# Conditioning-matrix products in bursts of two slabs, with an eight-buffer raw ring, in a conditioned hybrid decoder step

## The chip, the core and the metric

One Trainium2 chip, one of its cores. The metric is the device time of one execution of the whole step in microseconds (us), as the median of several runs. An execution that the profiler recorded supplies the rows; its span is the time from its first to its last instruction.

## The reference, cut to what matters

One decoder layer and a final RMSNorm are applied to 256 prompt tokens and 8 single-token samples. The nine modulation vectors (`mod`) come from the conditioning vector `c` through one large matrix, `ada_w` (2048 x 18432), here called the conditioning matrix.

```python
mod = (jax.nn.silu(c) @ ada_w + ada_b).reshape(n, N_SUBLAYERS, N_MOD, 1, D_MODEL)
h = modulate(rmsnorm(x, ffn1_norm), mod[:, 0, 0], mod[:, 0, 1])
x = x + FFN_RES * mod[:, 0, 2] * swiglu(h, ffn1_w_gate, ffn1_w_up, ffn1_w_down)
h = modulate(rmsnorm(x, mix_norm), mod[:, 1, 0], mod[:, 1, 1])
proj = h @ w_in
...
mixed = jnp.concatenate([y_ssm.reshape(n, l, D_SSM), y_pool], axis=-1).astype(x.dtype)
x = x + mod[:, 1, 2] * (mixed @ w_out)
h = modulate(rmsnorm(x, ffn2_norm), mod[:, 2, 0], mod[:, 2, 1])
x = x + FFN_RES * mod[:, 2, 2] * swiglu(h, ffn2_w_gate, ffn2_w_up, ffn2_w_down)
```

All arithmetic is float32. Between `w_in` and `w_out` one half of the channels goes through a state-space mixer (called S5) and the other through a pooling mixer.

## The kernel before

**Tokens and weights.** The 256 prompt tokens and 8 samples stand together as 264 moving columns. The weights (gate, up and down of both feed-forward blocks, `w_in`, `w_out`) are streamed once from HBM in slabs of 128 x 1024 float32 (512 KB), each of which holds eight 128 x 128 weight tiles. To keep float32 accuracy a slab is split into a high and a low part (`Stream.split`, lines 186 to 196: ScalarE copies to `hi`, line 190; VectorE computes `lo` = raw - hi, line 192), and each tile is multiplied in three passes: hi by Xh, hi by Xl, lo by Xh (`mm3`, lines 404 to 406). A weight slab is thus 24 matmuls of 264 columns.

**The conditioning matrix.** Its slabs go through the same stream but are not split. `sc` holds silu(c) as a stationary operand of 32 columns, and the slab itself is the moving operand. Four matmuls, each to its own group of 32 array columns and 32 PSUM partitions, make one step. For modulations 2 to 8 (`ada_step`, line 304) a step takes one of the 16 slices of the contraction, 2048 columns wide, which arrive as two 512 KB slabs; so here one slab of the title is a pair of DMAs, 7 x 16 = 112 of them. For modulations 0 and 1 (`ada0_step`, line 317) the columns are cut into five stages (`STG`), so that the first feed-forward block can begin before the whole of them is there: 8, 8, 16, 16 and 16 slabs of 512 KB. After the last slice VectorE transposes the PSUM tile (line 314 or 333) and `ada_fin` adds the bias; there is one PSUM tile for this work (`psa`, bufs=1), so the next modulation waits for the transposition of the last.

**Order.** All slabs, weights ("w") and conditioning ("a", and "b" for the further DMAs of a step), stand in one list, `ent`, in the order in which they are used. `Stream` issues their DMAs on SyncE's queue (SP) into a ring of 5 raw buffers; entry i waits until entry i-5 was used. When the matmuls need a further weight slab, `prep` first carries out every "a" entry that stands before it:

```python
    def fill(self):
        while self.dma < len(self.entries) and (self.dma < self.rb or self.used[self.dma - self.rb]):
            ...
    def prep(self):
        while self.is_ada():
            self.ada()
```

Up to three split slabs are kept ready. `w_units` and the table `pos` spread the conditioning steps over the weight slabs: in the first feed-forward block one step to some three weight slabs (modulations 4, 3, 2, 5), in the mixer stage (`win`, `wout`) one to some 1.3 (modulations 7, 6), in the beginning of the second block one to some 2.3 (modulation 8). The framework that builds the program may reorder instructions on an engine by its own plan, except where `keep_in_program_order` or a manual schedule forbids it.

**The S5 part** (`s5_v`, `s5_e`, `s5_y`) runs inside the second half of `win`: VectorE and ScalarE copy `u` into `V` (line 982), TensorE makes `E` from it (line 998), VectorE scans.

Of the kernel before, what the change touches and what calls it, by code (L numbers as in the profile page):

```python
# [21 lines left out]
KT = D // P  # L22
# [22 lines left out]
FV = 10  # L45
FIN = ((0, 1), (1, 1), (2, 2), (10, 2), (4, 2), (6, 2), (12, 2), (8, 2), (14, 2))
SG = 4
N1 = 3
STG = ((0, 2), (2, 4), (4, 8), (8, 12), (12, 16))

# [33 lines left out]
def ada0_units(s):  # L84
    a, b = STG[s]
    n = b - a
    if n == 1:
        return [((kt, kt + 1, kt + 2, kt + 3), (0, 1)) for kt in range(0, KT, 4)]
    if n <= 2:
        return [((kt, kt + 1), (0, 1)) for kt in range(0, KT, 2)]  # L90
    if n <= 4:
        return [((kt,), (0, 1)) for kt in range(KT)]
    return [((kt,), (i,)) for i in range(2) for kt in range(KT)]
# [116 lines left out]
def build(nc, tc, I, O):  # L210
    ctx = ExitStack()
    V, A, T, GP = nc.vector, nc.scalar, nc.tensor, nc.gpsimd
# [22 lines left out]
    wp = ctx.enter_context(tc.tile_pool(name="wp", bufs=1))  # L235
# [5 lines left out]
    def pt(shape, name, dt=F32):  # L241
        return pers.tile(list(shape), dt, tag=name, name=name)
# [33 lines left out]
    sc = pt([P, KT, 32], "sc")  # L276
# [18 lines left out]
    def ada_fin(at, mi, k0, k1):  # L295
        m = mods[mi][:, k0:k1, :]
        nk = k1 - k0
        add(m, at.rearrange("p (k b) -> p k b", b=32)[:, :, 0:NM], ada_b[:, mi, k0:k1].unsqueeze(2).broadcast_to([P, nk, NM]))
        if mi % 3 == 1:
            stt(m, m, 1.0, norms[:, mi // 3, k0:k1].unsqueeze(2).broadcast_to([P, nk, NM]), ALU.add, ALU.mult)  # L300
        elif mi in (2, 8):
            ts(m, m, 0.25)

    def ada_step(raws, mi, kt, stage):
        key = (mi, stage)
        if kt == 0:
            ada_ps[key] = psa.tile([P, 512], F32, tag="ada", name=f"ada{mi}_{stage}")
        ps = ada_ps[key]
        for j in range(4):
            T.matmul(ps[32 * j:32 * j + 32, :], lhsT=sc[:, kt, :], rhs=raws[j // 2][:, (j % 2) * 512:(j % 2 + 1) * 512],  # L310
                     start=(kt == 0), stop=(kt == KT - 1))
        if kt == KT - 1:
            at = wp.tile([P, 512], F32, tag="adaT", name=f"adaT{mi}_{stage}", bufs=1)
            V.transpose(out=at, in_=ps)  # L314
            ada_fin(at, mi, 0, KT)

    def ada0_step(raws, s, kts, ms):
        a, b = STG[s]
        n = b - a
        w = 32 * n  # L320
        if kts[0] == 0 and ms[0] == 0:
            ada_ps[s] = psa.tile([P, 512], F32, tag="ada", name=f"ada0_{s}")
        ps = ada_ps[s]
        r = raws[0][:, 0:len(kts) * len(ms) * 4 * w].rearrange("p (t m j c) -> p t m j c", t=len(kts), m=len(ms), j=4)
        for t, kt in enumerate(kts):
            for j in range(4):
                o = ps[32 * j:32 * j + 32, ms[0] * w:(ms[-1] + 1) * w].rearrange("p (m c) -> p m c", c=w)
                mm = T.matmul(o, lhsT=sc[:, kt, :], rhs=r[:, t, :, j, :], start=(kt == 0), stop=(kt == KT - 1))  # L328
                if s == 0:
                    tc.keep_in_program_order(mm)  # L330
        if kts[-1] == KT - 1 and ms[-1] == 1:
            at = wp.tile([P, 512], F32, tag="adaT", name=f"adaT0_{s}", bufs=1)
            tr = V.transpose(out=at[:, 0:2 * w], in_=ps[:, 0:2 * w])
            if s == 0:
                tc.keep_in_program_order(tr)
            for i in range(2):
                ada_fin(at[:, w * i:w * i + w], i, a, b)
            hooks["stage"](s)

    hooks = {}  # L340
    ent = []

    def ada_units(mi, kt):
        ent.append(("a", I["ada"][mi - 2, kt, 0], 2, (ada_step, mi, kt, None)))
        ent.append(("b", I["ada"][mi - 2, kt, 1]))

    def ada0_unit(s, i):
        ent.append(("a", I[f"ada0_{s}"][i], 1, (ada0_step, s) + ada0_units(s)[i]))

    def w_units(names, steps, first, last):  # L350
        us = [I[name][u] for name in names for u in range(I[name].shape[0])]
        pos = [first + (last - first) * i / max(1, len(steps)) for i in range(len(steps))]
        si = 0
        for u, ap in enumerate(us):
            while si < len(steps) and pos[si] <= u:
                ada_units(*steps[si])
                si += 1
            ent.append(("w", ap))
        while si < len(steps):
            ada_units(*steps[si])  # L360
            si += 1

    def steps(*ms):
        return [(mi, kt) for mi in ms for kt in range(KT)]

    for i in range(len(ada0_units(0))):
        ada0_unit(0, i)
# [3 lines left out]
    for s in range(len(STG) - 1):  # L371
        nu = SM * 2 * (STG[s][1] - STG[s][0]) // CH
        na = len(ada0_units(s + 1))
        k = 0
        for u in range(nu):
            if s == 0 and u == 0:
                ent.append(("w", I["w1"][u0 + u]))
            while k < na and k * (nu - 1) <= u * na:
                ada0_unit(s + 1, k)
                k += 1  # L380
            if s > 0 or u > 0:
                ent.append(("w", I["w1"][u0 + u]))
        while k < na:
            ada0_unit(s + 1, k)
            k += 1
        u0 += nu
    pos = {}
    s_a = steps(4, 3, 2, 5)
# [2 lines left out]
    for u in range(u0, n1):  # L391
        for s in pos.get(u, []):
            ada_units(*s)
        ent.append(("w", I["w1"][u]))
# [2 lines left out]

    for q in range(4):
        nc.sync.dma_start(out=x[:, 4 * q:4 * q + 4, :], in_=I["x"][:, 4 * q:4 * q + 4, :])
    st = Stream(nc, wp, ent, 5, 3)  # L400

    def mm3(ps, w, xh, xl, start, stop):
        hi, lo = w
# [266 lines left out]
    def first_block(pool, gh, gl, rb, n):  # L670
        pe2 = pse.tile([P, 2, 512], F32, tag="E", name=f"fe{cnt[0]}", bufs=1)
        pss = [bank() for _ in range(n - 2)] + [pe2[:, 0], pe2[:, 1]]
        for kt in range(KT):
            for ps in pss:
                mm3(ps[:, 0:NX], st.get(), gh[kt], gl[kt], kt == 0, kt == KT - 1)
            if kt == 2:
                rstd(rb)
        out = []
        for i, ps in enumerate(pss):
            g = pool.tile([P, N], F32, tag=f"fb{i}", name=f"fb{cnt[0]}_{i}", bufs=1)  # L680
            s8 = pool.tile([P, NM], F32, tag=f"fs{i}", name=f"fs{cnt[0]}_{i}", bufs=1)
            A.copy(out=s8, in_=ps[:, N:NX])
            mul(g, ps[:, 0:N], rb)
            A.activation(out=g[:, 0:SEQ], in_=g[:, 0:SEQ], func=AF.Identity, bias=s8[:, 0:1])
            add(g[:, SEQ:N], g[:, SEQ:N], s8[:, 1:9], GP)
            out.append(g)
        return out
# [57 lines left out]
    def ffn(shift, gs, gate, nm, first, gx, after):  # L745
        with ExitStack() as es:
# [5 lines left out]
            if first:  # L752
                def mid():
                    for _ in range(N1):
                        st.ada()
# [124 lines left out]
    with tc.tile_pool(name="mix", bufs=1) as mp:  # L880
        mixed = mp.tile([P, KT, N], F32, tag="mixed", name="mixed")
        with tc.tile_pool(name="poolp", bufs=1) as qp:
# [53 lines left out]
            pss = first_block(qp, X1[0], X1[1], rb, FBI)  # L936
            for a in range(0, KT, SG):
                for kt in range(a, a + SG):
                    one(kt)
                samples(a, a + SG)  # L940
            tc.keep_in_program_order(nc.sync.dma_start(out=pw, in_=I["poolw"]))

            def u_tile(hook=None):
                ps = bank()
                for kt in range(KT):
                    mm3(ps[:, 0:N], st.get(), Xh[:, kt, 0:N], Xl[:, kt, 0:N], kt == 0, kt == KT - 1)
                    if hook is not None:
                        hook(kt)
                return ps
# [6 lines left out]
            for mt in range(FBI, 8):  # L956
                ps = u_tile()
# [5 lines left out]
            ps = u_tile()  # L963
# [4 lines left out]
        with tc.tile_pool(name="s5p", bufs=1) as sp:  # L968
# [100 lines left out]
            for ft in range(1, NFT):  # L1069
# [5 lines left out]
                ps = u_tile(hook)  # L1075
# [30 lines left out]
            while plan:  # L1106
                a = plan.pop(0)
# [36 lines left out]
    with tc.tile_pool(name="fin", bufs=1) as fp:  # L1144
        rb = fp.tile([P, N], F32, tag="rb", name="rbf")
        rbp = rstd(rb)
        for a, n in FIN:
            o = fp.tile([P, 2, N], F32, tag="o", name=f"o{a}", bufs=len(FIN))
            for i in range(n):
                kt = a + i  # L1150
# [90 lines left out]


def program(L):
    nc = bacc.Bacc("TRN2", target_bir_lowering=False, num_devices=1)
    I = {k: nc.dram_tensor(k, a.shape, F32, kind="ExternalInput").ap() for k, a in L.items()}
    O = {k: nc.dram_tensor(k, s, F32, kind="ExternalOutput").ap() for k, s in OUTS.items()}
    with tile.TileContext(nc) as tc:
        build(nc, tc, I, O)
    nc.finalize()
    return nc  # L1250
# [21 lines left out]
```

## Time and profile before

| | |
|---|---|
| median of 3 runs | 2087.66 us (2086.51 to 2089.89) |
| span of the profiled execution | 2090.6 us, mean granted TensorE clock 0.986 of full |
| TensorE matmul (PE), busy | 2033.3 us, 97% of the span |
| VectorE (DVE), ScalarE (ACT), GpSimd (POOL) | 58%, 40%, 20% |
| DMA | 476 MB, 228 GB/s on average; queues q1 and q10 (hardware_dynamic, of SP and ScalarE), q8 and q14 (instruction) |

The profiled execution's own time is its span, 2090.6 us; the page shows nothing outside it, and it stands 2.9 us above the median of the runs. Busy shares of PE count a matmul until its modelled end, so that neighbours overlap; what a stream of matmuls costs is read from the distance of their starts. A matmul with float32 operands (the conditioning products) stands in the records twice, the three-pass ones once. A releaser behind an arrow (`<-`) is what ended the idle time before the row.

### The profile page before, as it was taken

The numbers are of one execution on the slowest core, as the hardware profiler recorded it, in microseconds if no ns is written. First come the engines' busy times: TensorE is split into PE (matmuls) and PEld (weight loads), VectorE is DVE, ScalarE is ACT, GpSimd is POOL, SyncE is SP. The second block draws the span as 40 slices with busy tenths as digits, with TensorE's granted clock in tenths as the row PEclk, the third lists the DMA queues.
The fourth block names the chain that finished last, engine by engine and source line by source line (L and its number), as shares of the span: only waits on it lengthen the run. The fifth ranks groups of instructions, "written<-read, shape, count | busy, mean of one in ns | idle before, by whom it ended". The sixth has DMA issues, their size and how long they took to land.

```text
span 2090.6 us, 41113 instructions
## 1 busy us (share of the span) xinstructions
PE 2033.3 (97%) x16856; PEld 1870.3 (89%) x16856; DVE 1212.7 (58%) x1978; ACT 842.3 (40%) x1258; POOL 410.6 (20%) x713
## 2 busy tenths in 40 slices
PE   6999999999999999999988899999999999999997
PEld 5788999899999989998766698899999999999997
DVE  4665855754444454467789776545555555554555
ACT  4332434433333333355445355433334333334343
POOL 0000100330764068043345332000000000000012
PEclk9999999999999999999989999999999999999998
DMA  8888777777676776777844656875555555555552
GB/s 321 314 296 286 246 261 252 286 267 250 229 247 231 258 252 234 267 261 251 314 151 178 219 205 219 283 273 182 180 175 180 182 187 175 182 182 175 179 181 103
DMA packets 135292, 476.43 MB, mean 228 GB/s; under 512 B 15160, under 2 KB 20152, under 8 KB 134840
## 3 DMA queue, kind: packets, MB, share of 16 engines
q1 hardware_dynamic: 134384, 473.07, 64.6%
q8 instruction: 132, 2.16, 0.4%
q10 hardware_dynamic: 720, 0.75, 0.1%
q14 instruction: 56, 0.46, 0.1%
HBM read 471.20 MB, written 3.01 MB: 227 GB/s over the span
## 4 chain that ended last, share of the span: by engine, by line
PE 71%; issue 11%; POOL 8%; DVE 7%; DMA 2%; ACT 1%; SPq 0%; POOLq 0%; ACTq 0%; DVEq 0%
PE mm L404 22%; PE mm L406 21%; PE mm L405 21%; PE ada_None L310 3%; POOL xu L215 2%; DVE lo L192 2%; PE ada L328 2%; POOL yt L215 1%; DVE V L982 1%; POOL X L215 1%; DMA raw<-ada 1%; POOL acc L215 1%; POOL h L215 1%; DVE S L215 1%; PE E L998 1%
## 5 line engine op out<-in xcount | busy, mean ns | idle before, releaser
L192 DVE TENSOR_TENSOR lo<-raw,hi 128x1024 fp32r<-128x1024 f32 x591 | 733.5, 1241 | 610.4 <-ACT hi L190 584.5
L190 ACT CAST hi<-raw 128x1024 fp32r<-128x1024 f32 x592 | 619.7, 1047 | 1000.6 <-PE mm L405 777.9
L404 PE MATMUL mm<-Xh,hi 128*128 128x264 f32 (+1 forms) x3168 | 922.8, 292 | 2.4 <-ACT Xh L735 1.7
L405 PE MATMUL mm<-Xl,hi 128*128 128x264 f32 (+1 forms) x3168 | 910.6, 288 | 0.0
L406 PE MATMUL mm<-Xh,lo 128*128 128x264 f32 (+1 forms) x3168 | 906.6, 287 | 1.7 <-DVE lo L192 1.5
L404 PEld LDWEIGHTS mm<-Xh,hi 128*128 128x128 f32 x3168 | 600.6, 190 | 77.3 <-issue 59.8
L406 PEld LDWEIGHTS mm<-Xh,lo 128*128 128x128 f32 x3168 | 602.8, 191 | 8.8 <-issue 5.6
L405 PEld LDWEIGHTS mm<-Xl,hi 128*128 128x128 f32 x3168 | 602.5, 190 | 7.9 <-issue 7.6
L404 PE MATMUL mm<-ah,hi 128*128 128x264 f32 x1408 | 404.3, 287 | 0.0
L406 PE MATMUL mm<-ah,lo 128*128 128x264 f32 x1408 | 400.7, 285 | 0.0
L405 PE MATMUL mm<-al,hi 128*128 128x264 f32 x1408 | 398.8, 283 | 0.0
L404 PEld LDWEIGHTS mm<-ah,hi 128*128 128x128 f32 x1408 | 264.9, 188 | 21.0 <-issue 15.9
L405 PEld LDWEIGHTS mm<-al,hi 128*128 128x128 f32 x1408 | 265.3, 188 | 0.0
L406 PEld LDWEIGHTS mm<-ah,lo 128*128 128x128 f32 x1408 | 264.7, 188 | 0.0
L215 POOL TENSOR_TENSOR acc<-acc,sq 128x264 f32<-128x264 f32 x42 | 45.8, 1089 | 748.5 <-ACT sq L655 748.5
L310 PE MATMUL ada_None<-raw,sc 128*32 128x512 f32 x896 | 129.0, 608 | 8.2 <-DVE adaT_None L314 5.0
L232 DVE SCALAR_TENSOR_TENSOR x<-mm,mod,x 128x256 f32<-128x256 f32 x78 | 37.6, 482 | 42.1 <-PE mm L406 42.1
L215 DVE TENSOR_TENSOR s<-s,mm 128x264 f32<-128x264 f32 x68 | 29.1, 428 | 55.7 <-PE mm L406 55.7
L328 PE MATMUL ada<-raw,sc 128*32 128x256 f32 (+1 forms) x640 | 43.8, 374 | 14.0 <-DMA raw<-ada 13.9
L215 POOL TENSOR_TENSOR xu<-X,apow 128x128 f32<-128x128 f32 x96 | 53.6, 579 | 3.8
L215 POOL TENSOR_TENSOR s<-s,partBuT 128x264 f32<-128x264 f32 x7 | 5.3, 755 | 219.4 <-DVE partBuT L215 203.0
L310 PEld LDWEIGHTS ada_None<-raw,sc 128*32 128x32 f32 x896 | 19.3, 108 | 29.8 <-DMA raw<-ada 9.3
(303 smaller groups left out, 1471.6 us busy)
## 6 DMA issues: line engine op xcount, KB each, us to landing
raw<-w SPq DMA_DIRECT2D x528, 512.0 KB, 3.8
raw<-ada SPq DMA_DIRECT2D x288, 512.0 KB, 5.2
raw<-win SPq DMA_DIRECT2D x32, 512.0 KB, 5.1
raw<-wout SPq DMA_DIRECT2D x32, 512.0 KB, 4.3
x<-x SPq DMA_DIRECT2D x4, 528.0 KB, 5.7
xin<-x SPq DMA_DIRECT2D x16, 132.0 KB, 3.7
y<-o SPq DMA_DIRECT2D x7, 264.0 KB, 2.7
Cm<-Cm SPq DMA_DIRECT2D x1, 1024.0 KB, 5.8
```

The costliest lines, as they stand in the source:

```text
L190: c = self.nc.scalar.copy(out=hi, in_=raw)
L192: e.tensor_tensor(out=lo, in0=raw, in1=hi.bitcast(F32), op=ALU.subtract)
L215: return e.tensor_tensor(out=out, in0=a, in1=b, op=op)
L232: return e.scalar_tensor_tensor(out=out, in0=a, scalar=s, in1=b, op0=op0, op1=op1)
L310: T.matmul(ps[32 * j:32 * j + 32, :], lhsT=sc[:, kt, :], rhs=raws[j // 2][:, (j % 2) * 512:(j % 2 + 1) * 512], start=(kt == 0), stop=(kt = ...
L328: mm = T.matmul(o, lhsT=sc[:, kt, :], rhs=r[:, t, :, j, :], start=(kt == 0), stop=(kt == KT - 1))
L404: T.matmul(ps, lhsT=hi, rhs=xh, start=start, stop=False)
L405: T.matmul(ps, lhsT=hi, rhs=xl, start=False, stop=False)
L406: T.matmul(ps, lhsT=lo, rhs=xh, start=False, stop=stop)
L982: e(out=v[32 * tau:32 * tau + 32, q, 64 * tau:64 * tau + n], in_=u[32 * q:32 * q + 32, 0:n])
L998: T.matmul(E[:, ri, q * 72:(q + 1) * 72], lhsT=bx[:, ri, q].rearrange("p a b -> p (a b)"), rhs=v[:, q, 192:N], start=True, stop=True)
```

## The change

`AB = 2` steps of the conditioning product now make one entry of the stream: `ada_step` takes four DMAs and does eight matmuls in a row, `ada0_steps` takes two slabs in a row (the first stage keeps single ones). The lists of steps are halved (`steps`), so that a burst comes after twice as many weight slabs. The ring of raw buffers grows from 5 to 8, which takes 12 KB more of each SBUF partition; for this the scratch for DMA descriptors is set to 1024 bytes.

```diff
+AB = 2
+RB = 8
...
-    def ada_step(raws, mi, kt, stage):
+    def ada_step(raws, mi, k0, stage):
...
-        for j in range(4):
-            T.matmul(ps[32 * j:32 * j + 32, :], lhsT=sc[:, kt, :], rhs=raws[j // 2][:, (j % 2) * 512:(j % 2 + 1) * 512],
-                     start=(kt == 0), stop=(kt == KT - 1))
-        if kt == KT - 1:
+        for kt in range(k0, k0 + AB):
+            for j in range(4):
+                T.matmul(ps[32 * j:32 * j + 32, :], lhsT=sc[:, kt, :],
+                         rhs=raws[2 * (kt - k0) + j // 2][:, (j % 2) * 512:(j % 2 + 1) * 512],
+                         start=(kt == 0), stop=(kt == KT - 1))
+        if k0 + AB == KT:
...
+    def ada0_steps(raws, s, i):
+        for r, u in zip(raws, ada0_units(s)[i:]):
+            ada0_step(r, s, *u)
...
     def ada_units(mi, kt):
-        ent.append(("a", I["ada"][mi - 2, kt, 0], 2, (ada_step, mi, kt, None)))
-        ent.append(("b", I["ada"][mi - 2, kt, 1]))
-
-    def ada0_unit(s, i):
-        ent.append(("a", I[f"ada0_{s}"][i], 1, (ada0_step, s) + ada0_units(s)[i]))
+        us = [I["ada"][mi - 2, k, h] for k in range(kt, kt + AB) for h in range(2)]
+        ent.append(("a", us[0], len(us), (ada_step, mi, kt, None)))
+        ent.extend(("b", u) for u in us[1:])
+
+    def ada0_unit(s, i, n=1):
+        ent.append(("a", I[f"ada0_{s}"][i], n, (ada0_steps, s, i)))
+        ent.extend(("b", I[f"ada0_{s}"][j]) for j in range(i + 1, i + n))
...
     def steps(*ms):
-        return [(mi, kt) for mi in ms for kt in range(KT)]
+        return [(mi, kt) for mi in ms for kt in range(0, KT, AB)]
...
             while k < na and k * (nu - 1) <= u * na:
-                ada0_unit(s + 1, k)
-                k += 1
+                ada0_unit(s + 1, k, AB)
+                k += AB
...
-    st = Stream(nc, wp, ent, 5, 3)
+    st = Stream(nc, wp, ent, RB, 3)
...
-    nc = bacc.Bacc("TRN2", target_bir_lowering=False, num_devices=1)
+    nc = bacc.Bacc("TRN2", target_bir_lowering=False, num_devices=1, dynamic_dma_scratch_size=1024)
```

The diff shifts the line numbers below it, by up to ten: lines 310, 314, 328, 404 and 982 of the kernel before are 313, 318, 336, 414 and 992 of the changed one. Three places show what the program makes of it.

TensorE, first feed-forward block, the first step of modulation 4 (`ada_None` is its PSUM tile, each row two matmuls; `mm` the accumulator of a weight product). Before:

```order
L405 MATMUL mm_2585<-Xl,hi_2498 128x264
L406 MATMUL mm_2585<-Xh,lo_2499 128x264
L310 MATMUL ada_None<-raw_2434,sc 32x512 x2
L310 MATMUL ada_None<-raw_2468,sc 32x512 x2
L404 MATMUL mm_2599<-Xh,hi_2532 128x264
L405 MATMUL mm_2599<-Xl,hi_2532 128x264
```

In the changed program:

```order
L415 MATMUL mm_2591<-Xl,hi_2504 128x264
L416 MATMUL mm_2591<-Xh,lo_2505 128x264
L313 MATMUL ada_None<-raw_2398,sc 32x512 x2
L313 MATMUL ada_None<-raw_2400,sc 32x512 x2
L313 MATMUL ada_None<-raw_2406,sc 32x512 x2
L313 MATMUL ada_None<-raw_2440,sc 32x512 x2
L414 MATMUL mm_2605<-Xh,hi_2538 128x264
L415 MATMUL mm_2605<-Xl,hi_2538 128x264
```

Two steps stand side by side, and the next burst follows after 144 weight matmuls instead of 72. All 56 bursts of modulations 2 to 8 look like this.

TensorE, first feed-forward block, third stage of modulations 0 and 1 (`ada_2`), two slabs of one entry in the changed program:

```order
L414 MATMUL mm_782<-Xh,hi_661 128x264
L336 MATMUL ada_2_648<-raw_576,sc 32x256 x4
L415 MATMUL mm_782<-Xl,hi_661 128x264
L416 MATMUL mm_782<-Xh,lo_662 128x264
L414 MATMUL mm_790<-Xh,hi_661 128x264
L415 MATMUL mm_790<-Xl,hi_661 128x264
L416 MATMUL mm_790<-Xh,lo_662 128x264
L414 MATMUL mm_790<-Xh,hi_661 128x264
L415 MATMUL mm_790<-Xl,hi_661 128x264
L416 MATMUL mm_790<-Xh,lo_662 128x264
L414 MATMUL mm_798<-Xh,hi_711 128x264
L336 MATMUL ada_2_648<-raw_614,sc 32x256 x4
```

Here the framework's own order puts nine weight matmuls between the two, so they remain two bursts. Of the 28 pairs of the four later stages 18 are kept apart like this; 10 stand side by side (2 of the fourth stage, 8 of the fifth).

VectorE, S5 part, the end of modulation 7 (`V` and `u` as above, `mod_86` is modulation 7). Before:

```order
L982 COPY V_12038<-u_12348 32x64
L232 SCALAR_TENSOR_TENSOR y_12404<-y_12404,gy_12405 128x264
L314 STREAM_TRANSPOSE adaT_None<-ada_None 128x512
L232 SCALAR_TENSOR_TENSOR gy_12405<-y_12404,gy_12405 128x264
L215 TENSOR_TENSOR mod_86<-adaT_None,sm 128x160
```

In the changed program:

```order
L992 COPY V_12045<-u_12205 32x64
L318 STREAM_TRANSPOSE adaT_None<-ada_None 128x512
L194 TENSOR_TENSOR lo_12251<-raw_12085,hi_12250 128x1024
L217 TENSOR_TENSOR mod_86<-adaT_None,sm 128x160
L194 TENSOR_TENSOR lo_12281<-raw_12087,hi_12280 128x1024
```

The transposition now stands behind the `V` copies of the S5 group before. On TensorE 76 matmuls lie between the last step of modulation 7 and the first of modulation 6, where 25 did.

## Rows read from the trace of the kernel before

**Rows 1.** The page: busy engines (part 1) and the chain that ended last (part 4).
```profile
PE 2033.3 (97%) x16856; PEld 1870.3 (89%) x16856; DVE 1212.7 (58%) x1978; ACT 842.3 (40%) x1258; POOL 410.6 (20%) x713
...
PE 71%; issue 11%; POOL 8%; DVE 7%; DMA 2%; ACT 1%; SPq 0%; POOLq 0%; ACTq 0%; DVEq 0%
```

**Rows 2.** Stretches (us): length, PE, PEld, DVE, ACT, POOL busy (count), clock, DMA share, GB/s.
```profile
220.00:930.00 710.00, 708.08 (x5659) 643.65 (x5658) 373.78 (x525) 265.64 (x364) 236.48 (x428) 1.00 0.73 254
...
1000.00:1046.00 46.00, 46.00 (x343) 36.17 (x344) 36.60 (x103) 19.17 (x38) 15.04 (x25) 1.00 0.87 315
...
1060.00:1076.00 16.00, 11.01 (x70) 8.13 (x62) 12.08 (x20) 5.16 (x14) 9.53 (x15) 0.75 0.43 149
...
1108.00:1124.00 16.00, 12.55 (x137) 10.60 (x137) 15.74 (x29) 7.57 (x18) 9.55 (x16) 0.85 0.54 198
...
1400.00:2070.00 670.00, 670.00 (x5459) 670.00 (x5459) 358.91 (x520) 265.50 (x316) 15.70 (x13) 1.00 0.51 177
```

**Rows 3.** Timeline of PE around a step of modulations 2 to 8: start, length, row.
```profile
802.67 0.28 PE L406 MATMUL mm<-Xh,lo 128*128 128x264 f32 x1
802.88 1.07 PE L310 MATMUL ada_None<-raw,sc 128*32 128x512 f32 x8
803.88 0.39 PE L404 MATMUL mm<-Xh,hi 128*128 128x264 f32 x1
804.10 0.29 PE L405 MATMUL mm<-Xl,hi 128*128 128x264 f32 x1
```

**Rows 4.** Timeline of PE around steps of modulations 0 and 1.
```profile
20.42 1.08 PE L328 MATMUL ada<-raw,sc 128*32 128x128 f32 x32
...
32.99 0.64 PE L328 MATMUL ada<-raw,sc 128*32 128x128 f32 x16
...
188.91 0.28 PE L406 MATMUL mm<-Xh,lo 128*128 128x264 f32 x1
189.13 0.64 PE L328 MATMUL ada<-raw,sc 128*32 128x256 f32 x8
...
189.92 0.28 PE L405 MATMUL mm<-Xl,hi 128*128 128x264 f32 x1
```

**Rows 5.** Timeline of PE: the steps that wait inside for their second DMA.
```profile
372.74 1.05 PE L310 MATMUL ada_None<-raw,sc 128*32 128x512 f32 x4
374.29 1.05 PE L310 MATMUL ada_None<-raw,sc 128*32 128x512 f32 x4 [0.50 <-DMA raw<-ada]
...
982.23 1.05 PE L310 MATMUL ada_None<-raw,sc 128*32 128x512 f32 x4
984.18 1.05 PE L310 MATMUL ada_None<-raw,sc 128*32 128x512 f32 x4 [0.90 <-DMA raw<-ada]
...
1175.37 1.05 PE L310 MATMUL ada_None<-raw,sc 128*32 128x512 f32 x4
1177.96 1.05 PE L310 MATMUL ada_None<-raw,sc 128*32 128x512 f32 x4 [1.54 <-DMA raw<-ada]
...
1207.27 1.85 PE L310 MATMUL ada_None<-raw,sc 128*32 128x512 f32 x8
...
1305.05 2.25 PE L310 MATMUL ada_None<-raw,sc 128*32 128x512 f32 x8
...
1317.25 2.03 PE L310 MATMUL ada_None<-raw,sc 128*32 128x512 f32 x8
```

**Rows 6.** Timeline of SP (DMA issues) ahead of the step at 1305.05.
```profile
1301.51 0.81 SPq L153 DMA_DIRECT2D raw<-ada  x2
```

**Rows 7.** DMA issues of the page (part 6): count, KB each, median us to landing.
```profile
raw<-ada SPq DMA_DIRECT2D x288, 512.0 KB, 5.2
```

**Rows 8.** Timeline of DVE and PE at the end of modulation 7.
```profile
1068.41 0.70 DVE L314 STREAM_TRANSPOSE adaT_None<-ada_None 128x512 f32<-128x512 f32 x1
...
1069.17 1.93 PE L310 MATMUL ada_None<-raw,sc 128*32 128x512 f32 x8 [4.99 <-DVE adaT_None L314]
```

**Rows 9.** Timeline of PE at the start: the first weight matmul.
```profile
26.63 1.25 PE L404 MATMUL mm<-Xh,hi 128*128 128x264 f32 x4 [1.75 <-ACT Xh L735]
```

More of the change, by code (lines that the diff above doesn't have):

```diff
@@ L302, in ada_fin @@
             ts(m, m, 0.25)
-    def ada_step(raws, mi, kt, stage):
+    def ada_step(raws, mi, k0, stage):
         key = (mi, stage)
-        if kt == 0:
+        if k0 == 0:
             ada_ps[key] = psa.tile([P, 512], F32, tag="ada", name=f"ada{mi}_{stage}")
         ps = ada_ps[key]
-        for j in range(4):
-            T.matmul(ps[32 * j:32 * j + 32, :], lhsT=sc[:, kt, :], rhs=raws[j // 2][:, (j % 2) * 512:(j % 2 + 1) * 512],
-                     start=(kt == 0), stop=(kt == KT - 1))
-        if kt == KT - 1:
+        for kt in range(k0, k0 + AB):
[4 more added lines that the diff above has]
+        if k0 + AB == KT:
             at = wp.tile([P, 512], F32, tag="adaT", name=f"adaT{mi}_{stage}", bufs=1)
@@ L315, in ada_step, with ada0_step @@
             ada_fin(at, mi, 0, KT)
-    def ada0_step(raws, s, kts, ms):
+    def ada0_steps(raws, s, i):
+        for r, u in zip(raws, ada0_units(s)[i:]):
+            ada0_step(r, s, *u)
+    def ada0_step(raw, s, kts, ms):
         a, b = STG[s]
@@ L323, in ada0_step @@
         ps = ada_ps[s]
-        r = raws[0][:, 0:len(kts) * len(ms) * 4 * w].rearrange("p (t m j c) -> p t m j c", t=len(kts), m=len(ms), j=4)
+        r = raw[:, 0:len(kts) * len(ms) * 4 * w].rearrange("p (t m j c) -> p t m j c", t=len(kts), m=len(ms), j=4)
         for t, kt in enumerate(kts):
@@ L383, in build @@
         while k < na:
-            ada0_unit(s + 1, k)
-            k += 1
+            ada0_unit(s + 1, k, AB)
+            k += AB
         u0 += nu
```

## The prediction

> **What bounds the kernel now.** I read the page first, then stretches of the span, then the timeline of TensorE around the conditioning products. The page shows PE busy for 97% of the span, and 71% of the chain that ended last is its work [rows 1]. That average hides two kinds of stage. In 220 to 930, in 1000 to 1046 and in 1400 to 2070 us PE is busy nearly all the time and VectorE about half of it or at most four fifths [rows 2]: whatever is taken out of PE's stream there shortens the run by the same amount. In 1400 to 2070 us 5459 matmuls fill 670 us, 0.123 us from start to start; this is the beat of the three-pass products, against which I measure everything else. In the S5 part it is otherwise: from 1108 to 1124 us VectorE is busy 15.74 of 16 us and PE 12.55 [rows 2], so that there PE waits for VectorE and a shorter PE stream gives nothing.
>
> DMA has room on average. Its tightest long stretch is 1000 to 1046 us, 315 GB/s at a busy share of 0.87, and there PE still had no idle time [rows 2].
>
> **The change part by part.** *What a burst costs now.* Around a step of modulations 2 to 8 the last weight matmul before starts at 802.67 and the second one after it at 804.10 [rows 3]. Without the step these two starts would be two beats apart, 0.246 us, so the step costs 1.43 - 0.25 = 1.18 us. The same for a 256-column step of modulations 0 and 1: 189.92 - 188.91 - 0.25 = 0.76 us [rows 4]. Part of it is not work of the step but the price of going from one kind of product to the other and back.
>
> *What the second slab of a burst costs.* No step of modulations 2 to 8 has a neighbour in the trace, but at 20.42 us two 128-column steps of modulation 0 stand side by side: their 32 records take 1.08 us, where the 16 records of a single one take 0.64 us [rows 4]. The second one adds 0.44 us. It is two slices of 128 columns, as much as one slice of 256; the steps of modulations 2 to 8 are 512 wide, so for them I take 2 x 0.44 = 0.88 us. The bounds: not more than a burst of its own, 1.18 us; not less than 512 columns at the beat of the weight matmuls (0.123 us for 264), 0.24 us for each of the two records of a matmul, 0.48 us, if the four column groups run wholly side by side. I take 0.88 because its row is of the same instruction and the same four groups. The Trainium skill has a rule that speaks for the lower end: in TensorE: Matmul & The Clock Gate, section Back-to-back issue gap, N columns follow each other every N/2.4 + 2.5 ns, which would be an estimate of 0.43 us for the two records of a slab, and a saving of 56 x 0.75 = 42 us. The row at 20.42 us does not agree: it took about twice that for its columns.
>
> *Modulations 2 to 8.* Two bursts cost 2 x 1.18 = 2.36 us, a merged one 1.18 + 0.88 = 2.06, so 0.30 us less; 112 steps become 56 bursts, as the order shows. 56 x 0.30 = 16.8 us. Some five of them fall into the S5 part, where VectorE covers the gain: less 1.5, so **15.3 us**.
>
> *Modulations 0 and 1.* Of 28 pairs only 10 stand side by side in the order; 10 x (0.76 - 0.44) = **3.2 us**. The 18 others keep both bursts, and I give them nothing.
>
> *Waits inside a burst.* Six steps stop halfway for their second DMA [rows 5]. From first start to last end they take 2.60, 3.00, 3.64, 1.85, 2.25 and 2.03 us, where the step at 802.88 takes 1.07 [rows 3]: 15.37 - 6 x 1.07 = 8.95 us lost. The step at 1305.05 waited for slabs that were issued at 1301.51 [rows 6], and a slab lands a median 5.2 us after its issue [rows 7]. With a ring of 5 a slab is issued when the entry five places ahead is used. With 8 places, in the mixer stage (some 2.7 weight slabs and four conditioning DMAs to a round, 2.7 x 24 x 0.123 + 2.06 = 10.0 us) the look-ahead is 8/6.7 of a round, 12 us; before it was 5/3.3 of a round of 5.1 us, 7.6 us. In the second feed-forward block it is 8/8.5 of 15.3 us, 14 us instead of 9. The bursts of four release their buffers at once, but these serve the burst after, a whole round later. So most of these waits go; I take three quarters, **6.7 us**. The ends: none of it, or all 8.95.
>
> *The wait for the transposition.* At 1069.17 PE had stood 4.99 us until VectorE had transposed modulation 7, since it came to that only at 1068.41, behind the copies of `V` [rows 8]. In the changed order the last step of modulation 7 comes a step earlier, and 76 weight matmuls instead of 25 lie ahead of the first step of modulation 6, 9 us instead of 3. The transposition should be done by then. But this is the S5 part: VectorE was idle only 16 - 12.08 = 3.9 us in that stretch [rows 2], and more than that can't be won. **3.5 us**, between 0 and 5.
>
> *Nothing.* At the start eight slabs instead of five are under way at once, but the first weight matmul waits for ScalarE's Xh, not for a slab [rows 9]; that chain covers it, and if it moves with the slabs, no more than the 1.75 us of that wait is at stake. On SP the further DMAs of a burst stand in the queue behind the same releases as before, and nothing else that PE needs stands behind them for longer than a slab. The smaller scratch changes no instruction of the order.
>
> The sum is 15.3 + 3.2 + 6.7 + 3.5 = 28.7 us. Against the profiled execution's 2090.6 us that gives 2061.9; the median of the runs stands 2.9 us lower, 2087.66, and so I predict 2087.7 - 28.7 = **2059.0 us**.
>
> **The rivals.** *The waits stay.* The longer ring is eaten up by bursts that need four landed DMAs instead of two, and the S5 part keeps its length. For it: DMA was busy 0.87 in 1000 to 1046 us, and the round gets shorter. Against it: the look-ahead above. Only the merging is left, 18.5 us: 2069.2 us.
>
> *The burst costs as much as two.* If going from one slice to the next costs as much as going from one kind of product to the other, the merging saves nothing and only 10.2 us remain: 2077.5 us. Against it stands the row at 20.42 us; for it, that this row is of narrower steps.
>
> *The second slab costs the lower bound.* At 0.48 us a merged burst of modulations 2 to 8 saves 0.70 and one of modulations 0 and 1 0.76 - 0.24 = 0.52: 51 x 0.70 + 10 x 0.52 = 40.9 us, with the other terms 51.1: 2036.6 us. The Trainium skill's rule on the issue gap, cited above, is this case. The row at 20.42 us speaks against it.
>
> *Slower: the last slab of a burst comes late.* PE works in order, so in the mixer stage and the second feed-forward block (8 bursts for each of modulations 7, 6 and 8, 24 in all) it would stand at the head of each burst until the fourth DMA is there. At most that is a landing, 5.2 us [rows 7]: 24 x 5.2 = 125 us, and 2087.7 - 18.5 + 125 = 2194 us. It decides from 18.5 / 24 = 0.77 us for each burst on. It takes a DMA that can't carry the shorter rounds; the 315 GB/s at which PE didn't wait speak against it.
>
> *No change.* The S5 part and the start, whose order on VectorE and ScalarE also moved, give back what the merging wins; they would have to lose some 20 us of which I see no source.
>
> **How the numbers follow.** A measurement of this kernel can tell about 0.2%, 4.2 us, from no change. The forecast gets 0.62, the waits that stay 0.19, the full price 0.05, the lower bound 0.04, late slabs 0.05, no change 0.05. The first four are faster: 0.90; same 0.05; slower 0.05. The forecast with all of the waits gone, 5.0 from the transposition, 1.75 at the start and a second slab somewhat cheaper (0.75 us: 6.6 more from 51 bursts) is 2059.0 - 2.25 - 1.5 - 1.75 - 6.6 = 2047; a little of the cheaper case takes the lower end to 2044. Upward it holds 2069.2, and a second slab that costs 0.95 (3.6 us): 2073. What is left out is the four small cases, 0.19.
>
> **What would show it.** The steps of modulations 2 to 8 should come as 16 records of about 1.95 us (1.07 + 0.88), a burst cost of about 2.06 us by the starts around it, and there should be 56 of them. Of modulations 0 and 1, 18 pairs should still stand apart at 0.76 us each. Few bursts should be much longer than 1.95 us; the wait for the transposition near 1065 us should be gone, with the S5 part some 3 us shorter. From 1400 us on the distance to the end should be unchanged. I am wrong if the merged burst takes 2.4 or 1.5 us, if the bursts of the mixer stage wait for `raw`, or if the S5 part has grown.

## The result and the profile after

The changed kernel takes **2067.64 us** (median of four runs, 2065.83 to 2070.63) against 2088.77 us (2086.51 to 2092.73) of the kernel before: a ratio of 0.9885, 95% interval 0.9864 to 0.9906. Run again beside three of the experiments it took 2068.27 us against 2091.68, 0.9888 (0.9872 to 0.9905). So 21 to 23 us are gone, of the 28.7 that were forecast; 2059.0 was too low by 8.6 us, and the time lies in the range of 2044 to 2073.

The profiled execution has a span of 2063.9 us and was the fastest of its four (2065.83 us). A time is some 2 us longer than the span of the same execution, so the 2090.6 us of before, a span, answer to a time of about 2092.6, 4 us above that kernel's median; the 2.9 us ahead of the prediction compared a span with times. The two traces are 26.7 us apart, and the text says each time whether a number is of traces or of medians.

The page, parts 1 and 4, which answer to [rows 1]:

```profile
PE 2005.7 (97%) x16856; PEld 1871.6 (91%) x16856; DVE 1207.1 (58%) x1978; ACT 842.1 (41%) x1258; POOL 412.0 (20%) x713
...
PE 71%; issue 12%; POOL 9%; DVE 6%; ACT 1%; DMA 1%; POOLq 0%; ACTq 0%; DVEq 0%
```

PE has the same 16856 records and is busy 27.6 us less (2033.3 before): no work was left out, and the shares hardly move. What did move is in the stretches. Those of the changed kernel that answer to [rows 2], the first the first feed-forward block, the second the S5 part, the third the dense end:

```profile
220.00:919.40 699.40, 696.38 (x5658) 645.02 (x5657) 371.39 (x524) 265.48 (x364) 235.14 (x427) 1.00 0.74 258
1033.00:1142.00 109.00, 90.32 (x1060) 74.66 (x1060) 106.20 (x198) 54.19 (x124) 65.60 (x101) 0.87 0.46 159
1372.70:2042.70 670.00, 670.00 (x5459) 670.00 (x5459) 359.05 (x520) 265.64 (x316) 15.71 (x13) 1.00 0.54 174
```

The first does the matmuls that took 710.00 us in 699.40. The last is 670.00 us with 5459 matmuls in both kernels: nothing happens there. The S5 part took 114 us before, and VectorE is now busy 106.20 of its 109 us, 97%.

The timeline of TensorE in the changed kernel, in order of time: two waits at the start, a merged pair of modulation 1, a burst of modulation 4 to 5, the first burst after modulation 7, one of modulation 8:

```profile
38.63 0.39 PE L414 MATMUL mm<-Xh,hi 128*128 128x264 f32 x1 [0.69 <-ACT hi L192]
...
99.62 0.39 PE L414 MATMUL mm<-Xh,hi 128*128 128x264 f32 x1 [0.52 <-ACT hi L192]
...
196.91 0.28 PE L416 MATMUL mm<-Xh,lo 128*128 128x264 f32 x1
197.13 1.07 PE L336 MATMUL ada<-raw,sc 128*32 128x256 f32 x16
198.13 0.39 PE L414 MATMUL mm<-Xh,hi 128*128 128x264 f32 x1
198.36 0.28 PE L415 MATMUL mm<-Xl,hi 128*128 128x264 f32 x1
...
794.13 0.28 PE L416 MATMUL mm<-Xh,lo 128*128 128x264 f32 x1
794.34 1.92 PE L313 MATMUL ada_None<-raw,sc 128*32 128x512 f32 x16
796.19 0.40 PE L414 MATMUL mm<-Xh,hi 128*128 128x264 f32 x1
796.43 0.28 PE L415 MATMUL mm<-Xl,hi 128*128 128x264 f32 x1
...
1049.04 1.92 PE L313 MATMUL ada_None<-raw,sc 128*32 128x512 f32 x16
...
1282.64 1.92 PE L313 MATMUL ada_None<-raw,sc 128*32 128x512 f32 x16
```

A burst now costs 796.43 - 794.13 - 0.246 = 2.05 us, a merged pair 198.36 - 196.91 - 0.246 = 1.20 us. The burst at 1049.04 has no wait in its brackets: the 4.99 us of [rows 8] are gone. The burst at 1282.64 is the one that took 2.25 us for a single slab at 1305.05 [rows 5]. Its DMAs, in the timeline of SP:

```profile
1269.87 2.11 SPq L155 DMA_DIRECT2D raw<-ada  x4
```

All four were issued by 1271.98, 10.7 us ahead of the burst. Before, the two of a step were issued from 1301.51 to 1302.32, 2.7 us ahead of the step at 1305.05 [rows 5, 6]. The part on DMA issues of the page shows that a landing takes longer, a median 6.2 us against the 5.2 of [rows 7]:

```profile
raw<-ada SPq DMA_DIRECT2D x288, 512.0 KB, 6.2
```

The eight places alone don't explain this: with the same ring and single slabs (e1, below) the median is 4.6 us.

The waits of TensorE (what it waited for: us in total, times, longest):

```profile
PE E L1008 <- DVE V L992: 15.5, 14, 3.4
...
PE mm L416 <- DVE lo L194: 3.8, 8, 1.8
...
PE mm L1060 <- POOL ca L217: 2.9, 2, 1.6
...
PE mm L937 <- DMA pw<-poolw: 1.3, 1, 1.3
```

No line is left of `ada_None` waiting for `raw` or for the transposition. In their place other waits grew; they are counted below, in the section on the prediction.

**Where the time went, matmul by matmul.** The matmuls that are not conditioning products are 15320 in both kernels, in nearly the same order. The start of the k-th one (counted from 0) after less that of the k-th one before, from the two traces:

| k | start before, us | after less before, us | the stretch up to there |
|---|---|---|---|
| 60 | 37.23 | +1.75 | start |
| 600 | 129.14 | +3.97 | modulations 0, 1, pairs still apart |
| 1200 | 218.98 | -0.11 | the merged pairs |
| 6300 | 923.60 | -10.60 | 32 bursts of the first block |
| 7000 | 1032.99 | -12.55 | mixer stage ahead of the S5 part |
| 8100 | 1162.10 | -18.79 | S5 part |
| 8700 | 1238.78 | -22.51 | end of the mixer stage |
| 9900 | 1409.96 | -27.30 | bursts of modulation 8 |
| 15300 | 2072.83 | -27.30 | nothing more |

From 219 to 924 us the gain is 10.5 us, as much as 32 bursts at 0.33. Two other things lie in that stretch and cancel: the wait inside the step at 372.74 [rows 5], which had cost 1.7 us by the starts, is gone, and TensorE now waits twice for `lo` where VectorE is busy 9.55 of the 10 us from 380 to 390 (before, one wait of 0.34 us at 382.07):

```profile
383.28 0.39 PE L416 MATMUL mm<-Xh,lo 128*128 128x264 f32 x1 [1.76 <-DVE lo L194]
...
387.06 0.39 PE L416 MATMUL mm<-Xh,lo 128*128 128x264 f32 x1 [0.57 <-DVE lo L194]
```

At the start there is a loss.

### The profile page after: what moved, and what is told of

Read it like the earlier page. It is cut to its first block, busy times and chain, and to the rows that moved or that the text cites. A ratio compares the mean times of both kernels' runs of the same rounds, so it can differ in the third digit from the quotient of the medians.

```text
span 2063.9 us, 41107 instructions
## 1 busy us (share of the span) xinstructions
PE 2005.7 (97%) x16856; PEld 1871.6 (91%) x16856; DVE 1207.1 (58%) x1978; ACT 842.1 (41%) x1258; POOL 412.0 (20%) x713
## 4 chain that ended last, share of the span: by engine, by line
PE 71%; issue 12%; POOL 9%; DVE 6%; ACT 1%; DMA 1%; POOLq 0%; ACTq 0%; DVEq 0%
PE mm L414 22%; PE mm L416 21%; PE mm L415 21%; PE ada_None L313 3%; POOL xu L217 2%; POOL yt L217 2%; PE ada L336 2%; POOL X L217 1%; DVE lo L194 1%; DVE V L992 1%; POOL acc L217 1%; DVE S L217 1%; DMA raw<-ada 0%; PE E L1008 0%; POOL h L217 0%
## 5 line engine op out<-in xcount | busy, mean ns | idle before, releaser
L416 PEld LDWEIGHTS mm<-Xh,lo 128*128 128x128 f32 x3168 | 601.5, 190 | 10.6 <-DVE lo L194 6.3
L313 PE MATMUL ada_None<-raw,sc 128*32 128x512 f32 x896 | 109.3, 598 | 0.0
L313 PEld LDWEIGHTS ada_None<-raw,sc 128*32 128x32 f32 x896 | 23.8, 109 | 42.0 <-issue 35.0
```

Of the source, the lines that this page charges most:

```text
L416: T.matmul(ps, lhsT=lo, rhs=xh, start=False, stop=stop)
```

## Experiments

Each is the changed kernel but for the edit shown.

**e1: the ring alone.**

```diff
-AB = 2
+AB = 1
```

> Ring of 8 and the small scratch, bursts of one slab as before. Theory A (the ring takes the waits inside bursts, the merging saves only what two bursts cost more than one): the steps of modulations 2 to 8 stay at a cost of 1.18 to 1.19 us, none of them waits inside for its second DMA (before: 8.95 us in six), the wait for the transposition (4.99 us) stays because TensorE's order is nearly that of before. 5 to 9 us under the kernel before: 2080 to 2084. Theory B (the merging takes the waits as well, since half as many bursts meet a late slab, and the ring does nothing): within 2 us of the kernel before, 2087 to 2091, with waits inside bursts of several us. Theory C (a ring of 8 costs at the start, because eight slabs share the DMA engines there): the first weight matmuls come 1.5 us or more later than before, by 1.6 us at the 60th.

Measured: 2081.78 us (2081.18 to 2086.18) against 2093.19, 0.9956 (0.9944 to 0.9969). The steps stand at 1.19 us each, none waits inside for its second DMA, and of the waits of TensorE the transposition's is left:

```profile
PE ada_None L313 <- DVE adaT_None L318: 4.7, 1, 4.7
```

The k = 300 matmul starts at 76.08 us, before at 77.23. This lead of 1.15 us stands from k = 60 on and isn't the ring's: the granted clock of 22 to 34 us was 0.86 in e1 and 0.72 in the kernel before. In e3, which has eight places too and the clock of before there, k = 60 comes 0.2 us later than before. Theory A holds, B falls, and so does C: no trace shows a cost of eight slabs at once at the start.

**e2: the merging alone.**

```diff
-RB = 8
+RB = 5
...
-    nc = bacc.Bacc("TRN2", target_bir_lowering=False, num_devices=1, dynamic_dma_scratch_size=1024)
+    nc = bacc.Bacc("TRN2", target_bir_lowering=False, num_devices=1)
```

> Bursts of two slabs with the ring of 5 and the scratch of before. Theory A: bursts of 16 records cost 2.05 us where nothing is late, but a ring of 5 holds little beside a burst's four slabs, so that waits inside bursts stay or grow: 9 us or more over the changed kernel, 2077 to 2090. Theory B (the ring does nothing): 2067.6, within 2 us.

Measured: 2093.91 us (2088.39 to 2097.62) against 2093.19, 1.0005 (0.9993 to 1.0016): nothing is won, beyond even the upper end that Theory A gave. Most bursts do cost 2.05 us, but thirteen of those of 16 records cost 15.2 us more between them. One of modulation 8, in the timeline of SP and in that of TensorE:

```profile
1300.55 6.64 SPq L155 DMA_DIRECT2D raw<-ada  x3
1310.09 2.50 SPq L155 DMA_DIRECT2D raw<-w  x5
```

```profile
1306.59 1.91 PE L313 MATMUL ada_None<-raw,sc 128*32 128x512 f32 x12
1310.37 1.05 PE L313 MATMUL ada_None<-raw,sc 128*32 128x512 f32 x4 [1.87 <-DMA raw<-ada]
```

The burst's last DMA was issued at the end of the row of three, near 1307 us, when the burst had begun, and five weight slabs stood behind it until 1310.09. The waits of TensorE name two things that neither the kernel before nor the changed one has to this extent, the second inside the S5 part:

```profile
PE ada_None L313 <- DMA raw<-ada: 5.7, 6, 1.9
PE mm L1060 <- DVE S L217: 5.2, 1, 5.2
```

By the starts of the matmuls it is 8 us behind the changed kernel at k = 6600, 14.5 at 7000, 23.6 at 8400, 28.6 from 9900 on. Ring and merging are not two gains side by side: the merging is worth some 14 us (0.9956 to 0.9888) on the long ring and nothing on the short one.

**e3: modulations 2 to 8 alone.**

```diff
-                ada0_unit(s + 1, k, AB)
-                k += AB
+                ada0_unit(s + 1, k)
+                k += 1
...
-            ada0_unit(s + 1, k, AB)
-            k += AB
+            ada0_unit(s + 1, k)
+            k += 1
```

> The change without its part on modulations 0 and 1: their steps go one by one as before, modulations 2 to 8 in bursts of two slabs, ring of 8. In the profile of the changed kernel the 10 merged pairs save 3.3 us, and by the 60th weight matmul 1.6 to 2.8 us had been lost again. Theory A (a pair taken when its first half is due puts one more slab of 512 KB ahead of the weight slab; at 333 GB/s that is 1.57 us): the start loses nothing, the pairs win nothing, 2067 to 2069, the same as the changed kernel within 2 us. Theory C (the ring of 8 costs the start): the loss stays and the pairs' 3.3 us are missing, 2070 to 2073.

Measured: 2068.14 us (2068.03 to 2072.76), 0.9891 (0.9877 to 0.9904): the same as the changed kernel, as Theory A said. Its trace is 3.8 us ahead of that of the changed kernel at k = 600 and 0.3 behind at k = 1200: it has neither of the two waits for `hi` at 38.63 and 99.62 us, and not the pairs' gain.

**e4: pairs taken late.**

```diff
-            while k < na and k * (nu - 1) <= u * na:
+            while k < na and (k + AB - 1) * (nu - 1) <= u * na:
```

> The change, but a pair of modulations 0 and 1 is taken when its second half is due, not its first. Theory A (the early pair pushes back a weight slab at the start): the start's loss of 1.6 to 2.8 us goes and the pairs' gain stays, 2064 to 2066. Theory C (the ring of 8 costs the start): 2067.6 within 1.5 us.

Measured: 2065.5 us (2062.06 to 2068.62), 0.9872 (0.9858 to 0.9886). The interval overlaps those of the changed kernel, so a gain isn't shown. By the starts it is 1.8 us ahead at k = 1200 as hoped, but 0.06 at k = 9900. The lead is still 0.8 us at k = 7000 and 0.6 at k = 8100, so that less of it goes in the S5 part than before and behind it; in 383 to 386 us e4's granted clock was 0.51, where the changed kernel had 1.00. The waits at 38.63 and 99.62 are gone; one for `lo` at 95.05 grew from 0.50 to 1.27 us.

**e5: bursts of four slabs.**

```diff
-AB = 2
+AB = 4
```

> Bursts of four slabs (32 records of modulations 2 to 8, eight DMAs) in place of two, ring of 8. Theory A (a burst pays for the change of kind once and 0.87 us for each further slab; the ring must hold the burst and what comes after it): where nothing is late a burst costs 2.05 + 2 x 0.87 = 3.79 us instead of 2 x 2.05, 28 x 0.31 = 8.7 us less in all; but the burst takes all eight places, so that bursts in the mixer stage and the second feed-forward block wait inside, as bursts of four DMAs did with a ring of 5: slower than the changed kernel by 5 to 25 us. Theory D (the ring is long enough for any burst that it can hold): 8.7 us less than the changed kernel.

Measured: 2106.15 us (2101.58 to 2116.12) against 2091.68, 1.0077 (1.0053 to 1.0101): 38 us over the changed kernel. Where nothing is late a burst of 32 records costs 3.77 us (the one at 1198.62), so that a further slab is (3.77 - 2.05)/2 = 0.86 us, and Theory A's slope holds. But it is one of few: the median is 4.1 us, since the last DMA of most bursts comes some 0.3 us late (in the one at 303.67 it landed at 306.56, and the products that use it, due at 306.27, started at 306.60), and four bursts cost 7.2, 9.6, 8.8 and 10.8 us; the last one in the timeline of TensorE:

```profile
1311.91 2.78 PE L313 MATMUL ada_None<-raw,sc 128*32 128x512 f32 x24
1316.51 1.05 PE L313 MATMUL ada_None<-raw,sc 128*32 128x512 f32 x4 [1.82 <-DMA raw<-ada]
1320.46 1.92 PE L313 MATMUL ada_None<-raw,sc 128*32 128x512 f32 x4 [2.89 <-DMA raw<-ada]
```

Theory D falls; the loss is larger than A's 5 to 25 us.

**e6: bursts of four in the first block alone, pairs late.**

```diff
+AM = {2: 4, 3: 4, 4: 4, 5: 4, 6: 2, 7: 2, 8: 2}
...
-        for kt in range(k0, k0 + AB):
+        for kt in range(k0, k0 + AM[mi]):
...
-        return [(mi, kt) for mi in ms for kt in range(0, KT, AB)]
+        return [(mi, kt) for mi in ms for kt in range(0, KT, AM[mi])]
...
-            while k < na and k * (nu - 1) <= u * na:
+            while k < na and (k + AB - 1) * (nu - 1) <= u * na:
```

> Bursts of four slabs for modulations 2 to 5 alone, which lie in the first feed-forward block (DMA 0.73 busy there), bursts of two elsewhere; pairs of modulations 0 and 1 taken when their second half is due. Theory A: 32 bursts of 2.05 become 16 of 3.79, 16 x 0.31 = 5.0 us less in 220 to 900 us if the eight DMAs of a burst land in time, and 1 to 2 us less before 220 us: 4 to 7 us under the changed kernel. Theory E (a burst that fills the ring starves the weights behind it even at a DMA share of 0.73): TensorE waits for hi or lo after each burst or inside it, the gain is gone or turned into a loss of 1 us or more for each of the 16 bursts.

Measured: 2077.39 us (2074.76 to 2080.91), 0.9932 (0.9919 to 0.9944), 9 us slower than the changed kernel beside it: Theory E. The sixteen bursts cost a median 4.13 us, as much as the two of 2.05 that each replaces, and the loss goes beyond them: 14.5 us between k = 1200 and 6300 against e8's trace, of which the bursts are 71.5 - 32 x 2.05 = 5.9. (The profiled execution was e6's slowest, 2080.91 us, so the trace shows some 3.5 us more loss than the median has.) The worst burst, timeline of TensorE, then of SP:

```profile
391.05 2.78 PE L314 MATMUL ada_None<-raw,sc 128*32 128x512 f32 x24
394.55 1.05 PE L314 MATMUL ada_None<-raw,sc 128*32 128x512 f32 x4 [0.72 <-DMA raw<-ada]
396.77 1.05 PE L314 MATMUL ada_None<-raw,sc 128*32 128x512 f32 x4 [1.18 <-DMA raw<-ada]
```

```profile
380.24 12.56 SPq L156 DMA_DIRECT2D raw<-ada  x5
392.89 5.30 SPq L156 DMA_DIRECT2D raw<-w  x8
```

The eighth DMA goes out at the end of a row that began at 380.24 and ends at 392.80, after the burst's first start at 391.05, and then eight weight slabs at once.

**e7: a ring of 6.**

```diff
-RB = 8
+RB = 6
```

> The change with a ring of 6. With 5 the merging won nothing, with 8 about 19 us beyond the ring's own gain. Theory A (look-ahead in rounds: 6 places of 6.7 in a mixer round of 10.0 us are 9 us, against 12 us with 8 and 7.5 us with 5): some of the waits inside bursts stay, 3 to 10 us in all, and the time lies between: 6 to 16 us over the changed kernel. Theory F (it only takes a place or two beyond the burst): within 3 us of the changed kernel.

Measured: 2074.23 us (2071.04 to 2076.43), 0.9914 (0.99 to 0.9928), 6.0 us over the changed kernel, the low end of Theory A. But its profiled execution, its fastest, doesn't show A's mechanism: one burst is late by 1.7 us (at 980.35), and at k = 10200 the trace is 0.84 us ahead of that of e8 and level with that of the changed kernel. It loses 5.8 us in one place of the dense end, and this begins on ScalarE:

```profile
1675.47 0.39 ACT L773 ACTIVATE s<-mm 128x264 f32<-128x264 f32 x1 [2.00 <-PE mm L416]
1681.86 0.41 ACT L778 CAST ah<-s 128x264 fp32r<-128x264 f32 x1 [6.00 <-DVE s L217]
1682.17 2.93 ACT L192 CAST hi<-raw 128x1024 fp32r<-128x1024 f32 x3
```

In this kernel the framework put `ah` ahead of three splits that ran at once when it was through; it waits for VectorE's `s`, and that for the end of a product on TensorE. The Trainium skill says in Perfetto Trace Analysis, section Tensor Engine Instruction, that ACT, DVE and GPSIMD are "strict FIFO"; these rows agree, with 6.00 us. TensorE then stands 1.91 us for `hi` at 1683.27 and 0.74 for `lo` at 1684.53. The rest of the 5.8 us is the clock. The stretch behind these waits, in e7 and in e8 (the last number but two is the granted clock):

```profile
1684.00:1690.00 6.00, 5.47 (x25) 5.48 (x26) 2.74 (x3) 1.56 (x3) 0.00 (x0) 0.50 0.69 216
...
1684.00:1690.00 6.00, 6.00 (x51) 6.00 (x50) 3.37 (x4) 2.43 (x4) 0.00 (x0) 1.00 0.51 180
```

That is 26 matmuls fewer, 3.2 us at the beat. So most of what this trace loses comes from the framework's order and not from late slabs. What the slower executions of this kernel lose beyond that wasn't seen.

**e8: the changed kernel again.** No edit.

> The changed kernel itself, on the same chip as the three beside it: 0.987 to 0.991 of the kernel before.

Measured: 2068.27 us (2066.2 to 2068.93), 0.9888.

**e9: the scratch alone.**

```diff
-AB = 2
-RB = 8
+AB = 1
+RB = 5
```

> The kernel before with nothing but the smaller descriptor scratch: bursts of one slab, ring of 5. No theory gives the scratch a price, since no instruction moves: 0.998 to 1.002 of the kernel before. If it cost something, the ring's own gain would be larger than e1 showed, and TensorE would wait longer for slabs.

Measured: 2091.57 us against 2091.01, 0.9998 (0.9989 to 1.0008). No price of the scratch is seen, within 0.1%.

**e10: late pairs and a ring of 9.**

```diff
-RB = 8
+RB = 9
...
-            while k < na and k * (nu - 1) <= u * na:
+            while k < na and (k + AB - 1) * (nu - 1) <= u * na:
...
-    nc = bacc.Bacc("TRN2", target_bir_lowering=False, num_devices=1, dynamic_dma_scratch_size=1024)
+    nc = bacc.Bacc("TRN2", target_bir_lowering=False, num_devices=1, dynamic_dma_scratch_size=512)
```

> Pairs of modulations 0 and 1 taken late, as in e4, and a ring of 9 (scratch of 512). Theory A (with 8 places no burst waits any more, so a ninth has nothing left to take): 0.986 to 0.988 of the kernel before, as e4's 0.9872. Theory G (weights that were late, 1.8 us at 383 us of the changed kernel among them, gain from a longer ring): 0.983 to 0.985.

Measured: 2066.8 us (2065.13 to 2069.19), 0.9883 (0.9868 to 0.9898), not to be told from the changed kernel. Theory G falls: the wait at 383 us of the changed kernel is still there, 1.75 us long at 381.31. No version that was run is shown to beat the changed kernel.

## Why the prediction was right, and where not

*Modulations 2 to 8: right.* The steps of before cost a median 1.19 us, the bursts 2.05: 2 x 1.19 - 2.05 = 0.33 us each where 0.30 was forecast, 56 x 0.33 = 18.5 instead of 16.8 us. The second slab is 0.86 us, by the bursts of two and again by those of four, against 0.88 taken from the 128-column steps. The rival of the lower bound, 0.48 us, is out. Its condition holds all the same: four records of two column groups take 1.05 us [rows 5] and eight records of all four 1.07 [rows 3], so the groups do run side by side. What it had wrong is the beat: the records of the burst at 794.34 start four at a time, 0.43 us apart (794.34, 794.79, 795.22, 795.65), so 512 columns take 0.43 us for each of the two records of a matmul, not 0.24 as by the weight matmuls. Why they do, no run here shows. The Trainium skill's rule in TensorE: Matmul & The Clock Gate, section Back-to-back issue gap, would make an estimate of 0.43 us of a slab if each of its records were a single pass; the runs show 0.86, twice that.

*Modulations 0 and 1: right in the burst, wrong around it.* Ten pairs stand as 16 records and 18 apart at 0.76 us, as the order said; the ten are worth 2 x 0.763 - 1.197 = 0.33 us each, 3.3 us where 3.2 were forecast. But the part *Nothing* **failed at the start**. What it weighed there was the longer ring, and that costs nothing (e1, e3). What it overlooked is the loop that places the entries: a pair is taken when its first half is due, so one more slab stands ahead of a weight slab in the stretch where DMA is busiest. The two waits for `hi`, at 38.63 and 99.62 us in the changed kernel, stand at the same matmuls in e2, e7 and e8, which take pairs early too, and in none of e1, e3, e4, e6 and e10, which don't. By k = 1200 the 3.3 us are gone but for 0.11. Of the 1.75 us lost at k = 60 what lies ahead of the first of these waits, 0.9 to 1.0, is scatter: e8 is the same program, has the wait, and is 1.0 us earlier there.

*Waits inside a burst: right that the ring takes them, too small.* Three quarters of 8.95 us were booked; all of it is gone, already in e1, whose gain of 9 to 11 us by ratio and medians is of this size (8.5 between the traces, 1.1 of it at the start, by the clock). The look-ahead of 14 us worked out for the second feed-forward block is 12.8 us by the first DMA of the burst at 1282.64 (1282.64 - 1269.87).

*Transposition: right, too small.* The step cost 7.28 us before by the starts around it, 6.1 more than a step that doesn't wait (the wait of 4.99 and, after it, records of 1.93 instead of 1.07 us [rows 3, 8], with a granted clock of 0.50 from 1069 to 1071 us); 3.5 were booked, since VectorE's idle time seemed to allow no more than 3.9. VectorE transposes modulation 7 earlier, and the burst at 1049.04 finds it done; the view of its tile in the changed kernel:

```profile
L318 DVE STREAM_TRANSPOSE adaT_None<-ada_None x1: 717/717/717, 1040.4 to 1040.4; 128x512 f32<-128x512 f32 x1
```

It is the merging that moves it, since the wait stays in e1 and is gone in e2.

*What was late next: the largest error, and in another place.* 1.5 us were set aside, for the S5 part. In the traces the bursts cost 38.3 us less in all (the starts around them add up to 151.1 us before and 116.1 after for modulations 2 to 8; the pairs save 3.3), and 27.3 of it stays: 11.0 were given back. By stretches, from the same starts:

| stretch | bursts cost less by, us | gained, us | given back, us |
|---|---|---|---|
| up to k = 1200 | 3.3 | 0.1 | 3.2 |
| 1200 to 6300, first block | 12.2 | 10.5 | 1.7 |
| 6300 to 7000, mixer stage ahead of the S5 part | 7.2 | 2.0 | 5.2 |
| 7000 to 8100, S5 part | 7.7 | 6.2 | 1.4 |
| 8100 to 9900 | 7.9 | 8.5 | -0.6 |

In the S5 part the waits changed places: those for `V` went from 10.6 us to 15.5 and `ca` came to 2.9, while that for `gy`, 3.1 us, is gone. It gave back about what was booked, and became 5 us shorter where 3 were forecast. The **step that failed** is the reading of the mixer stage ahead of it, that whatever is taken out of TensorE's stream there shortens the run by as much. It gave back 5.2 us (e8 5.1, e3 5.4). In the middle of it TensorE had no idle time before, but the others had little either. The rows of before, then of about the same matmuls in the changed kernel:

```profile
991.00:1011.00 20.00, 20.00 (x138) 15.43 (x138) 18.24 (x68) 11.19 (x32) 7.18 (x14) 1.00 0.94 343
...
980.00:1000.00 20.00, 17.42 (x126) 13.10 (x126) 18.08 (x66) 12.12 (x34) 6.05 (x14) 1.00 0.86 333
```

VectorE was busy 18.24 of the 20 us and DMA 0.94 of them, more than the average of 1000 to 1046 us in [rows 2] shows. TensorE now comes sooner and waits for what these bring:

```profile
989.31 0.39 PE L414 MATMUL mm<-Xh,hi 128*128 128x264 f32 x1 [0.52 <-ACT Xh L735]
990.42 0.39 PE L415 MATMUL mm<-Xl,hi 128*128 128x264 f32 x1 [0.72 <-DVE Xl L217]
...
993.38 2.02 PE L937 MATMUL mm<-z,pw 128*128 128x264 f32 x8 [1.34 <-DMA pw<-poolw]
```

The load of `pw`, the pooling mixer's weights, stands in SP's queue behind two of a burst's DMAs:

```profile
983.03 4.42 SPq L155 DMA_DIRECT2D raw<-ada  x2
987.55 0.38 SPq L951 DMA_DIRECT2D pw<-poolw  x1
```

It went out 5.8 us ahead of the products that use it; before it was 7.3 us (997.2 to 1004.5), and nothing waited. The sentence that nothing else which TensorE needs stands behind the further DMAs for longer than a slab overlooked it. The waits of this stretch are 3.0 us more than before; the other 2 us of the 5.2 weren't traced to a cause.

*The sum.* Between the traces 28.7 us were forecast and 27.3 measured, but as two errors that cancel: the gains were forecast at 30.2 us before the 1.5 for the S5 part and are 38.3; what is given back was forecast at 1.5 and is 11.0. That the sum comes out so near is luck. Between medians it is 21 to 23 us: the traces flatter, as the profiled execution of after is its fastest and that of before stood 4 us above its median.

*The rival "the waits stay"* has the nearest time, 2069.2 us, and is nevertheless false: no wait inside a burst is left. Its price was wrong too. It took the merging's 18.5 us as safe with a ring that doesn't help; e2 is that case, and there the merging is worth nothing, since a burst of four DMAs on five places makes its own waits, 15.2 us of them, and starves the weights behind. *Slower* had the right mechanism, the last slab of a burst: in e2 it eats up the gain, and in e5 it shows in full. *The burst costs as much as two* and *no change* are out.

## What to carry to other kernels

A longer burst of one kind of product saves the price of changing over, but it wants its inputs landed together: count the ring in bursts, with the burst and the work until the next landing side by side. Here bursts of four DMAs lost all their gain on five places and had no late slab on eight (on six, one burst was 1.7 us late). The two edits were worth 9 us and nothing apart and 23 us together, so neither can be judged alone. A stretch where TensorE never stands still pays only as far as the others in it have room: read their shares over 20 us, not over the stage. An entry that is made larger also moves what stands behind it in the queue; ask when it becomes due by its last part, not by its first.

## What was not expected of the hardware

In the changed kernel a conditioning slab takes a median 6.2 us to land instead of 5.2 and still comes in time; the burst at 1282.64 had its last one issued 10.7 us ahead. In e1, with as many places, the median is 4.6 us. What makes the difference stays open.

A short wait can cost more than its length. In e6 TensorE stood 0.24 and 0.73 us for `X` at 563.53 and 564.92 us. The stretches around it in that kernel (the last number but two is the granted clock):

```profile
560.00:566.00 6.00, 5.03 (x41) 4.58 (x40) 3.15 (x5) 2.41 (x3) 5.45 (x13) 1.00 0.49 175
...
566.00:572.00 6.00, 6.00 (x31) 6.00 (x31) 1.99 (x3) 0.27 (x1) 2.60 (x5) 0.54 0.23 87
```

TensorE had been busy 5.03 of the 6 us; then the granted clock was 0.54, near the lower of its two levels (1.2 of 2.4 GHz), and TensorE, busy all of 566 to 572 us, did 31 matmuls in it, where the beat of 0.123 us gives 49. Against the changed kernel e6 lost 4.1 us there, between k = 3600 and 3750, with no burst of its own between the two. The changed kernel has no such dip in this block.

The end of e7 is a second case, above: TensorE busy 3.87 of 6 us (1678 to 1684), then a granted clock of 0.50. But not every such wait is followed by a fall: in the changed kernel TensorE was busy 3.52 of the 5 us from 378 to 383, in e4 3.24, and from 383 to 386 us the granted clock was 1.00 in the one and 0.51 in the other. Single traces of two kernels can therefore differ by 3 us for this alone.
